# Turning keys and values for chunked linear attention: from TensorE transposes to VectorE block transposes and transfers

## The chip, the core and the metric

The kernel runs on one core of one Trainium2 chip. The metric is the device time of one launch in microseconds (us), lower is better; a time shown is the median of several runs. The engines of the core are TensorE (PE, its weight loads PEld), VectorE (DVE), ScalarE (ACT), GpSimd (POOL) and SyncE (SP, which issues transfers here).

## What is computed

One decoder layer for 1088 tokens (a prompt of 1024 and 8 samples of 8 tokens). Behind a norm, one projection gives queries, keys and values for eight heads of width 128: four retention heads (r0 to r3) and four mLSTM heads (m0 to m3). Each head runs over chunks of 128 tokens. For a retention head:

```
def step(S, inp):
    qc, kc, vc = inp
    scores = jnp.einsum('bhnd,bhmd->bhnm', qc, kc) * dmat[None]
    out = (jnp.einsum('bhnm,bhmv->bhnv', scores, vc)
           + jnp.einsum('bhnd,bhdv->bhnv', qc, S) * xi[None, :, :, None])
    S_new = (S * chunk_decay[None, :, None, None]
             + jnp.einsum('bhmd,bhmv->bhdv', kc * zeta[None, :, :, None], vc))
    return S_new, out
```

The mLSTM heads do the same with a running maximum, a gate per token and a normaliser. An output projection, norms and a gated feed-forward network with a causal convolution follow.

## The kernel before

All arithmetic is float32. A projection product is three matmuls on high and low parts (line 160), of 128 x 128 weights by 272 token columns; a tensor of 128 output columns (a query, key or value of one head) takes four quarters of 24 such matmuls. Projections leave a tensor with head dimension on partitions and tokens on the free axis (`q`, `k`, `v`, 128 x 1088). The chunk matmuls need keys and values the other way round, with the tokens of a chunk on partitions. So `front` handles two chunks at a time: TensorE transposes the two key chunks (L632) and the two value chunks (L633) into one PSUM tile `x`, VectorE scales the keys from there into `kz` (L636 for m heads, L640 for r heads), ScalarE scales the values into `vts` (L644), and TensorE makes the scores `s` (L666). `pt` (L669, L672) is the masked score. `u` (L774) is the key-value product of a chunk, `o` (L779, L781) the output, `S` (L785, L787) the running state. Chunks 0 to 7 are the prompt's; chunk 8 holds the samples.

The order of instructions on each engine comes from the Tile scheduler: the program is written head by head, and matmuls of the next head's projection stand between those of a pair of chunks. `proj` (L463) runs the projections, `evac_rot`, `evac_norm` and `evac_copy` bring their results out of PSUM; `last["row", b]` remembers the instruction that completed quarter b. `finish_previous` lets out the closing steps of the head before, ordered behind such an instruction. An r head from r1 on projects q, k, then v (r0 and r1 have their values from the start), an m head q, k, v. Weights come through SP into `st_in` and are split into `wh_in` and `wl_in` (L144, L146) some projections ahead. SP issues its transfers in order; a transfer whose source is not ready holds what stands behind it. Tiles that share a tag share a buffer in turn.

At the start the norms of the input run beside the first projections: ScalarE squares input tiles (L233), VectorE adds them (L235 to L237), TensorE sums over partitions (`ssqb_pm`, L210), ACT and DVE make the factor `rb` (L211 to L217) and scale the rotary tables `tab` with it (L310). The rotary step L500 on block 0 of `q_r0` then frees the PSUM bank that quarter 3 of r0's query projection, `in0_3`, writes next.

Of the kernel before, what the change touches and what calls it, by code (L numbers as in the profile page):

```python
# [16 lines left out]
P = 128  # L17
# [3 lines left out]
NB = 8  # L21
# [71 lines left out]
def hybrid_layer_kernel(ctx: ExitStack, tc: tile.TileContext, a: dict, o: dict):  # L93
# [166 lines left out]
    def tok(name, rows=P, dt=F32):  # L260
        return tokp.tile([P, T], dt, tag="tok", name=name)[:rows, :]
# [29 lines left out]
    sums = [m2.tile([P, NB, 129], F32, tag=t, bufs=1, name=f"sums_{t}").rearrange("p s v -> p (s v)") for t in ("vx", "sb")]  # L291
    sqs = [tok(f"sq{i}").rearrange("p (k n) -> p k n", k=4) for i in range(2)]
    for b in range(5):
# [31 lines left out]
        return out  # L325

    def spread_tile(name):
        return m2.tile([P, NB * 129], F32, tag="vx", bufs=1, name=name)

    rbd = dr.tile([1, T], F32, name="rbd")  # L330

# [36 lines left out]
        nc.scalar.activation(ig, ig, AF.Identity, bias=vec[0:NH, V_BG + 1:V_BG + 2])  # L368

    def gate_consts():  # L370
        xst = m2.tile([P, X_N], F32, tag="vx", bufs=1, name="xst")
# [87 lines left out]


    yT = []

    def proj(*jobs, mid=None, done=None, banks=lambda i, b: psA, pair=False):  # L463

# [29 lines left out]
    def evac_rot(t, name):  # L494
        def f(b, ps):
            o0, n = BLK[b]
            sw = m2.tile([P, Q], F32, tag="sw", name=f"sw_{name}{b}")[:, :n]
            nc.scalar.activation(sw[0:64, :], ps[64:128, :], AF.Copy)
            nc.scalar.activation(sw[64:128, :], ps[0:64, :], AF.Copy)
# [56 lines left out]
    def mix_head(hd, ml):  # L556
# [3 lines left out]
        if hid == 0:  # L560
            vs = [tok(f"v_r{i}") for i in range(2)]
            proj(*((i, evac_copy(t), w) for i, t, w in zip(first, vs, wv)),
                 banks=alternate, pair=True)
            early.extend(vs)
        v = early.pop(0) if early else tok(f"v_{nm}")
        q, k = tok(f"q_{nm}"), tok(f"k_{nm}")
        if ml:
            ub = ub_tile(f"ub{hd}")
            row = urows[hd:hd + 1, :]
            nc.sync.dma_start(ub, bass.AP(row.tensor, row.offset, [[0, P], [1, UB]]))  # L570
            proj((16 + hd, evac_norm(q, 1.0), split_w(staged.pop(), f"in{16 + hd}")))
            row = last["row", 3]
            proj((20 + hd, evac_norm(k, SCALE)), banks=alternate)
            finish_previous(2, row)
            proj((24 + hd, evac_copy(v)))
            finish_previous(1, last["row", 3])
            finish_previous(2, last["row", 3])
        else:
            eq, ek = evac_rot(q, f"q{nm}"), evac_rot(k, f"k{nm}")
            if hd == 0:  # L580
                proj((0, eq, split_to(stage_w(a["wi"][0], "in0"), *first_q)), mid=pre_norm, banks=lambda i, b: psB)
                here["wq"] = mp.tile([P, 2, 2, 2 * P], F32, tag="wq", name="wq")
                proj((NH, ek))
            else:
                proj((hd, eq))
                row = last["row", 3]
                proj((NH + hd, ek), banks=alternate)
                finish_previous(2, row)
                if hd == 1:
                    finish_previous(3, last["row", 1])  # L590
                    finish_previous(3, last["row", 2])
            if hd == 0:
                token_norms()
            if hd > 1:
                proj((2 * NH + hd, evac_copy(v)))
                finish_previous(1, last["row", 3])
                finish_previous(2, last["row", 3])
# [12 lines left out]
        if hid >= NH - 1:  # L610
            j = 12 + hid + 1 if hid + 1 < 2 * NH else 28
# [5 lines left out]
        dec = m2.tile([P, 8], F32, tag="dec", name=f"dec_{nm}")  # L617

        own = []

        def front(cs):

            c0, L = cs[0], len(cs)
            nmc = f"{nm}{c0}"
            px = bank(psB, 512, f"x_{nmc}").rearrange("p (j i n) -> p j i n", j=2, i=2)
            if c0 < 8:
                kc, vc = ([chunk(t, c) for c in cs] for t in (k, v))
            else:
                own.append(spread_tile(f"sp_{nm}"))
                kc, vc = ([spread_copy(t, own[0][:, i * P:(i + 1) * P])] for i, t in enumerate((k, v)))  # L630
            for i, c in enumerate(cs):
                nc.tensor.transpose(px[:, 0, i, :], kc[i], ident)  # L632
                nc.tensor.transpose(px[:, 1, i, :], vc[i], ident)  # L633
            kz = m2.tile([P, 2, P], F32, tag="kz", name=f"kz_{nmc}")
            if ml:
                nc.vector.tensor_tensor(kz[:, :L], px[:, 0, :L, :],  # L636
                                        cols[:, c0:c0 + L, NH + hd].unsqueeze(2).broadcast_to([P, L, P]), ALU.mult)
            else:
                zc = C_ZE + hd + (0 if c0 < 8 else NH)
                nc.vector.tensor_scalar(kz[:, :L], px[:, 0, :L, :], rc(zc, 1), None, ALU.mult)  # L640
# [915 lines left out]
```

## Time and profile before

| what | value |
|---|---|
| median of 3 runs | 1310.88 us (1310.76 to 1311.48) |
| the profiled execution's own time | 1311.53 us |
| its span in the trace | 1309.7 us |
| TensorE's mean granted clock | 0.997 of full speed |
| PE busy | 1296.0 us, 99% of the span |
| PEld / DVE / ACT / POOL busy | 98% / 76% / 46% / 33% |
| chain that ended last | PE 96%, DVE 2%, DMA 1%, ACT 1% |

The rows below come from the profiled execution, whose time is 0.65 us above the median. An engine's busy share is an average over stages; the stage tables and waits below tell which engine sets the pace where.

### The profile page before, as it was taken

The numbers are of one execution on the slowest core, as the hardware profiler recorded it, in microseconds if no ns is written. First come the engines' busy times: TensorE is split into PE (matmuls) and PEld (weight loads), VectorE is DVE, ScalarE is ACT, GpSimd is POOL, SyncE is SP. The second block draws the span as 40 slices with busy tenths as digits, with TensorE's granted clock in tenths as the row PEclk, the third lists the DMA queues.
The fourth block names the chain that finished last, engine by engine and source line by source line (L and its number), as shares of the span: only waits on it lengthen the run. The fifth ranks groups of instructions, "written<-read, shape, count | busy, mean of one in ns | idle before, by whom it ended". The sixth has DMA issues, their size and how long they took to land.

```text
span 1309.7 us, 26782 instructions
## 1 busy us (share of the span) xinstructions
PE 1296.0 (99%) x10501; PEld 1285.9 (98%) x10501; DVE 998.3 (76%) x2002; ACT 600.0 (46%) x1144; POOL 430.8 (33%) x564
## 2 busy tenths in 40 slices
PE   9999999999999999999999999999999999999996
PEld 9999999999999999999999999999999999999996
DVE  7774766657767655678999878787787888897678
ACT  7544433323433346455744434343443455543563
POOL 0354341758882000001334321222222214593002
PEclk9999999999999999999999999999999999999998
DMA  7344443567783124233144433444334469533363
GB/s 262 109 139 150 148 147 116 181 193 236 239 267 123 51 66 152 69 103 134 53 153 163 150 120 120 149 138 144 115 125 156 132 207 311 175 95 95 95 222 137
DMA packets 90784, 194.46 MB, mean 148 GB/s; under 512 B 13849, under 2 KB 39065, under 8 KB 90146
## 3 DMA queue, kind: packets, MB, share of 16 engines
q1 hardware_dynamic: 78210, 150.30, 34.4%
q0 software_dynamic: 12160, 41.95, 9.7%
q8 instruction: 82, 1.34, 0.4%
q10 hardware_dynamic: 288, 0.50, 0.1%
q14 instruction: 44, 0.36, 0.1%
HBM read 136.21 MB, written 56.50 MB: 147 GB/s over the span
## 4 chain that ended last, share of the span: by engine, by line
PE 96%; DVE 2%; DMA 1%; ACT 1%; issue 0%; SPq 0%
PE in L160 30%; PE out L160 7%; PE up_S L1130 6%; PE up_S L1129 6%; PE up_S L1128 6%; PE dn L1355 5%; PE dn L1356 5%; PE dn L1357 5%; PE up_A L1129 5%; PE up_A L1128 5%; PE up_A L1130 5%; PE up_A L1180 1%; PE up_A L1179 1%; PE up_A L1178 1%; DVE facc L1432 1%; PE s_r L666 1%
## 5 line engine op out<-in xcount | busy, mean ns | idle before, releaser
L160 PE MATMUL in<-hh,wh_in 128*128 128x272 f32 x960 | 277.8, 292 | 0.8 <-ACT hh L227 0.8
L160 PE MATMUL in<-hh,wl_in 128*128 128x272 f32 x960 | 277.4, 291 | 0.2 <-DVE wl_in L146 0.2
L160 PE MATMUL in<-hl,wh_in 128*128 128x272 f32 x960 | 277.1, 291 | 0.0
L160 PEld LDWEIGHTS in<-hh,wh_in 128*128 128x128 f32 x960 | 180.1, 188 | 2.8 <-issue 1.4
L160 PEld LDWEIGHTS in<-hh,wl_in 128*128 128x128 f32 x960 | 180.3, 188 | 1.4 <-issue 1.0
L160 PEld LDWEIGHTS in<-hl,wh_in 128*128 128x128 f32 x960 | 179.8, 188 | 0.9 <-issue 0.7
L144 ACT ACTIVATE wh_up<-st_up 128x1024 fp32r<-128x1024 f32 x84 | 80.5, 960 | 168.8 <-PE up_S L1129 97.1
L146 DVE TENSOR_TENSOR wl_up<-st_up,wh_up 128x1024 fp32r<-128x1024 f32 x84 | 96.0, 1144 | 9.9 <-ACT wh_up L144 9.9
L1102 DVE TENSOR_TENSOR Uv<-Uv,up_S 128x272 f32<-128x272 f32 (+1 forms) x200 | 66.4, 374 | 45.5 <-PE up_S L1130 45.5
L1283 DVE TENSOR_TENSOR rb<-rb 128x544 fp32r<-128x544 f32 x78 | 75.6, 974 | 28.7 <-ACT rb L1282 28.1
L1304 POOL TENSOR_TENSOR wd<-wd 128x512 f32<-128x512 f32 x44 | 74.5, 1715 | 47.0 <-DMA wd<-in_wd 20.0
L1282 ACT ACTIVATE rb<-rb 128x544 fp32r<-128x544 f32 x78 | 50.7, 651 | 82.2 <-DMA rb<-bd 71.2
L823 POOL TENSOR_TENSOR tab<-tab 128x256 f32<-128x256 f32 x104 | 79.1, 771 | 11.9 <-DMA tab<-in_wu 7.4
L1163 POOL TENSOR_TENSOR act<-act 128x544 f32<-128x544 f32 x40 | 63.4, 1586 | 58.0 <-DMA bd<-act 36.2
L1093 POOL MEMSET Ug<- 128x2 f32 x22 | 2.2, 99 | 221.5 <-DMA xr<-in_x 100.2
L1143 DVE SCALAR_TENSOR_TENSOR c<-Uv,vec,c 128x1024 f32<-128x1024 f32 (+1 forms) x88 | 68.5, 783 | 8.5 <-ACT c L1141 8.5
L1143 DVE SCALAR_TENSOR_TENSOR c<-Ug,vec,c 128x1024 f32<-128x1024 f32 x88 | 69.1, 825 | 0.0
L823 POOL TENSOR_TENSOR wq<-wq 128x256 f32<-128x256 f32 x56 | 47.8, 863 | 45.8 <-DMA wq<-in_wu 43.6
L144 ACT ACTIVATE wh_in<-st_in 128x1024 fp32r<-128x1024 f32 (+2 forms) x31 | 31.9, 1028 | 57.0 <-PE in L160 56.1
L1141 ACT ACTIVATE c<-Ug,vec 128x1024 f32<-128x1024 f32 (+1 forms) x44 | 34.6, 834 | 45.5 <-DVE Ug L1106 43.9
L823 POOL DMA_DIRECT2D tab<-in_wu x52 | 36.8, 713 | 33.1 <-DVE k_r L500 21.7
L1130 PE MATMUL up_S<-T1h,wl_up 128*128 128x272 f32 x160 | 46.4, 290 | 0.0
(557 smaller groups left out, 4652.8 us busy)
## 6 DMA issues: line engine op xcount, KB each, us to landing
rb<-bd SPq DMA_DIRECT2D x76, 272.0 KB, 2.8
st_up<-sd SPq DMA_DIRECT2D x40, 512.0 KB, 3.9
bd<-act SPq DMA_DIRECT2D x33, 544.0 KB, 3.3
st_in<-in_wi SPq DMA_DIRECT2D x31, 512.0 KB, 3.8
tab<-in_wu POOLq DMA_DIRECT2D x52, 256.0 KB, 5.3
sd<-tab POOLq DMA_DIRECT2D x26, 512.0 KB, 3.6
st_up<-in_wu SPq DMA_DIRECT2D x24, 512.0 KB, 3.2
wd<-in_wd SPq DMA_DIRECT2D x44, 256.0 KB, 5.1
```

What stands on the lines that cost most here:

```text
L144: act = nc.scalar.activation(hi, x, AF.Copy)
L146: last["split"] = act, eng.tensor_tensor(lo, x, hi.bitcast(F32), ALU.subtract)
L160: last["product", b] = nc.tensor.matmul(ps, u[:, k * P:(k + 1) * P], x[b // 2][k // 4][v][:, k % 4, qcols(b)], start=k == term == 0, stop= ...
L823: last["sums"] = f(*args)
L1102: nc.vector.tensor_tensor(o_, o_ if x is None else c(x), c(ps), ALU.add)
L1128: nc.tensor.matmul(ps, wh[:, c], xh[:, k, n], start=k == 0, stop=False)
L1129: nc.tensor.matmul(ps, wh[:, c], xl[:, k, n], start=False, stop=False)
L1130: nc.tensor.matmul(ps, wl[:, c], xh[:, k, n], start=False, stop=k == 3)
L1143: last["conv"] = nc.vector.scalar_tensor_tensor(c, u(i), cw(i), c, ALU.mult, ALU.add)
L1283: nc.vector.tensor_tensor(lo, x, hi.bitcast(F32), ALU.subtract)
L1304: last[out] = nc.gpsimd.tensor_tensor(quad(p, out), quad(p, x), quad(p, y), op)
L1355: nc.tensor.matmul(t, wh[:, ms], ah, start=k == 0, stop=False)
```

## The change

Chunks 0 to 7 of keys and values are no longer transposed by TensorE. `flip` does it when a projection's odd quarter is out of PSUM: for a half of 512 tokens VectorE transposes 32 x 32 blocks (L474 of the changed kernel), SP writes the result (256 KB) to a bounce buffer in DRAM (L475), and after the second half SP reads it back in four transfers of 32 partitions (128 KB each, in runs of 512 bytes, L479), which put every block in its final place: values back into `v`, keys into a new tile `kt` (for m heads the place in `yT` that the head's output takes later). The scaling of keys into `kz` (L670, L675) and of values into `vts` (L680) reads these tiles instead of PSUM. `kz` is ordered behind the query's last quarter on VectorE, and for r heads `vts` behind the query's last quarter on ScalarE. The sample chunk 8 is still transposed by TensorE.

R heads from r2 on now project k, v, q, r1 k, q, and m heads k, v, q; the closing steps of the head before are let out at other points, the weights are loaded in the new order, and some tiles have other buffers (`xst` and one of the `sums` tiles move, `ub` shares with `kt`). Over the whole program TensorE has 128 transposes fewer, VectorE 32 block transposes more, and SP 96 transfers more (32 writes, 64 reads); the numbers of ACT's and POOL's instructions stay. From the projection `in29` on, every engine's order is as it was.

```diff
+    def flip(dst, src, name):
+        bounce = dr.tile([2, P, CH4], F32, tag="bounce", bufs=4, name=f"bounce_{name}")
+        def f(b):
+            if b % 2 == 0:
+                return
+            half = slice(b // 2 * CH4, (b // 2 + 1) * CH4)
+            x = src[:, half]
+            d = m2.tile([P, CH4], F32, tag="flip", bufs=1, name=f"flip_{name}{b // 2}") if dst is src else dst[:, half]
+            nc.vector.transpose(d.rearrange("p (j c b) -> p c j b", j=4, c=4), x.rearrange("p (c j a) -> p c j a", c=4, j=4))
+            nc.sync.dma_start(bounce[b // 2], d)
+            if b == 3:
+                rows_ = bounce.rearrange("h (i a) n -> a (h i) n", i=4)
+                for j in range(4):
+                    nc.sync.dma_start(dst[32 * j:32 * j + 32, :8 * P].rearrange("p (g n) -> p g n", g=8),
+                                      rows_[:, :, j * P:(j + 1) * P])
+        return f
...
         if ml:
...
-            proj((16 + hd, evac_norm(q, 1.0), split_w(staged.pop(), f"in{16 + hd}")))
+            proj((20 + hd, evac_norm(k, SCALE), split_w(staged.pop(), f"in{20 + hd}")), done=flip_k)
             row = last["row", 3]
-            proj((20 + hd, evac_norm(k, SCALE)), banks=alternate)
+            proj((24 + hd, evac_copy(v)), banks=alternate, done=flip(v, v, f"v_{nm}"))
             finish_previous(2, row)
-            proj((24 + hd, evac_copy(v)))
-            finish_previous(1, last["row", 3])
-            finish_previous(2, last["row", 3])
+            finish_previous(3, row)
+            proj((16 + hd, evac_norm(q, 1.0)), banks=alternate)
+            finish_previous(3, last["row", 0])
...
-            for i, c in enumerate(cs):
-                nc.tensor.transpose(px[:, 0, i, :], kc[i], ident)
-                nc.tensor.transpose(px[:, 1, i, :], vc[i], ident)
...
             if ml:
-                nc.vector.tensor_tensor(kz[:, :L], px[:, 0, :L, :],
-                                        cols[:, c0:c0 + L, NH + hd].unsqueeze(2).broadcast_to([P, L, P]), ALU.mult)
+                with tc.issue_after(kz_after[c0 // 4].ins) if c0 < 8 else nullcontext():
+                    nc.vector.tensor_tensor(wide(kz[:, :L]), kx, cols[:, c0:c0 + L, NH + hd].unsqueeze(2).unsqueeze(3)
+                                            .broadcast_to([P, L, 4, 32]), ALU.mult)
...
-                nc.scalar.activation(vt[:, i, :P], px[:, 1, i, :], AF.Copy, scale=rcol[:, c:c + 1])
+                with tc.issue_after(vts_after[c0 // 4].ins) if c0 < 8 and not ml else nullcontext():
+                    nc.scalar.activation(vt[:, i, :P].rearrange("p (i b) -> p i b", i=4), vx[:, i], AF.Copy, scale=rcol[:, c:c + 1])
```

The order of the engines shows three places. The first is the start of the program, in the stretch that leads to the rotary step on `q_r0`'s block 0. VectorE's rows there before:

```order
L235 TENSOR_TENSOR sq0_143<-sq0_143,sq1_144 128x1088
L212 TENSOR_SCALAR rb_84<-ssqb_pm0_498 128x272
L236 TENSOR_TENSOR sq0_143<-sq0_143 128x544
L215 SCALAR_TENSOR_TENSOR sums_sb_142<-sums_sb_142,rb_84 128x272
L217 SCALAR_TENSOR_TENSOR rb_84<-sums_sb_142 128x272
L146 TENSOR_TENSOR wl_in12_843<-st_in12_840,wh_in12_842 128x1024
L310 TENSOR_TENSOR tab_81<-tab_81,rb_84 128x272 x2
L212 TENSOR_SCALAR rb_84<-ssqb_pm1_539 128x272
L500 TENSOR_TENSOR q_r0_467<-in0_0_473,tab_81 128x272
```

And VectorE's rows of the same stretch in the changed kernel, whose L525 is the rotary step:

```order
L474 STREAM_TRANSPOSE flip_v_r11_482<-v_r1_256 128x4x4x32
L212 TENSOR_SCALAR rb_84<-ssqb_pm0_522 128x272
L235 TENSOR_TENSOR sq0_141<-sq0_141,sq1_142 128x1088
L215 SCALAR_TENSOR_TENSOR sums_1_144<-sums_1_144,rb_84 128x272
L236 TENSOR_TENSOR sq0_141<-sq0_141 128x544
L217 SCALAR_TENSOR_TENSOR rb_84<-sums_1_144 128x272
L146 TENSOR_TENSOR wl_in12_875<-st_in12_872,wh_in12_874 128x1024
L310 TENSOR_TENSOR tab_81<-tab_81,rb_84 128x272 x2
L212 TENSOR_SCALAR rb_84<-ssqb_pm1_563 128x272
L525 TENSOR_TENSOR q_r0_489<-in0_0_497,tab_81 128x272
```

The first L212 went ahead of L235, and a block transpose ahead of both. ScalarE's rows that feed this stretch, before:

```order
L233 ACTIVATE sq1_144<-x3_106 128x1088
L233 ACTIVATE sq0_143<-x3_106 128x1088
L498 ACTIVATE sw_qr00_508<-in0_0_473 64x272
L499 ACTIVATE sw_qr00_508<-in0_0_473 64x272
L211 ACTIVATE sums_sb_142<-ssqb_pm0_498,eps_69 128x272
L213 ACTIVATE sums_sb_142<-sums_sb_142 128x272
L214 ACTIVATE sums_sb_142<-sums_sb_142 128x272
```

And ScalarE's rows there in the changed kernel:

```order
L233 ACTIVATE sq1_142<-x3_106 128x1088
L523 ACTIVATE sw_qr00_532<-in0_0_497 64x272
L524 ACTIVATE sw_qr00_532<-in0_0_497 64x272
L211 ACTIVATE sums_1_144<-ssqb_pm0_522,eps_69 128x272
L213 ACTIVATE sums_1_144<-sums_1_144 128x272
L233 ACTIVATE sq0_141<-x3_106 128x1088
L214 ACTIVATE sums_1_144<-sums_1_144 128x272
```

The last square, which L235 on VectorE reads, went behind four other ScalarE instructions.

The second place is the start of head m1's chunks on TensorE (`yt` are transposes of the finished head's output, `in18` and `in22` projections of m2). Before:

```order
L710 MATMUL yt_m0s_4485<-cst_80,on_m0s_4045 128x128
L632 MATMUL x_m10_4495<-cst_80,k_m1_4077 128x128
L633 MATMUL x_m10_4495<-cst_80,v_m1_4075 128x128
L632 MATMUL x_m10_4495<-cst_80,k_m1_4077 128x128
L633 MATMUL x_m10_4495<-cst_80,v_m1_4075 128x128
L666 MATMUL s_m10_4511<-q_m1_4076,k_m1_4077 128x128 x2
L632 MATMUL x_m12_4516<-cst_80,k_m1_4077 128x128
L633 MATMUL x_m12_4516<-cst_80,v_m1_4075 128x128
L632 MATMUL x_m12_4516<-cst_80,k_m1_4077 128x128
L633 MATMUL x_m12_4516<-cst_80,v_m1_4075 128x128
L666 MATMUL s_m12_4532<-q_m1_4076,k_m1_4077 128x128 x2
```

In the changed kernel the same place reads:

```order
L746 MATMUL yt_m0s_4509<-cst_80,on_m0s_4049 128x128
L702 MATMUL s_m10_4530<-q_m1_4080,k_m1_4081 128x128 x2
L702 MATMUL s_m12_4546<-q_m1_4080,k_m1_4081 128x128 x2
L160 MATMUL in22_0_4756<-hh_00_145,wh_in22_4752 128x272
L160 MATMUL in22_0_4756<-hh_00_145,wl_in22_4753 128x272
```

The eight transposes are gone; 19 matmuls of `in22` then stand ahead of the first `u`, where 23 of `in18` stood.

The third place is SP's order around the turned tensors of m1 in the changed kernel:

```order
L790 DMA out_cs<-sb_m0_3844 1024x1x128
L475 DMA bounce_k_m1_4082<-yT2_845 128x512
L644 DMA sb_m1_4515<-in_sc 128x8x128
L646 DMA sb_m1_4515<-in_sn 128x8x1
L132 DMA st_in26_4869<-in_wi 128x1024
L479 DMA yT2_845<-bounce_k_m1_4082 32x8x128 x4
L475 DMA bounce_v_m1_4201<-flip_v_m10_4260 128x512
L475 DMA bounce_v_m1_4201<-flip_v_m11_4315 128x512
L132 DMA st_in18_5047<-in_wi 128x1024
L479 DMA v_m1_4079<-bounce_v_m1_4201 32x8x128 x4
L132 DMA st_in23_5180<-in_wi 128x1024
```

Before, `out_cs`, the two loads of `sb` and three weight loads stood there and nothing else; the bounce's writes and reads now stand between them.

## Rows read from the trace of the kernel before

**Rows 1.** Busy us of each engine by stretch, with its instructions, TensorE's clock, DMA share, GB/s.

```profile
340.00:388.00 48.00, 48.00 (x408) 47.34 (x408) 33.75 (x105) 17.70 (x54) 40.96 (x58) 1.00 0.75 245
...
436.00:495.00 59.00, 59.00 (x495) 58.34 (x493) 40.43 (x123) 26.04 (x61) 0.00 (x0) 1.00 0.17 56
```

**Rows 2.** What TensorE waited for, in us, times and longest, the longest of four rows.

```profile
PE ssqb_fin L210 <- ACT facc_sq L1367: 1.3, 1, 1.3
```

**Rows 3.** The chain that ended last, at m1's first chunks: start us, us, what.

```profile
337.90 0.87 PE in L160 x7
...
339.32 0.11 PE x_m L632
...
339.76 0.45 PE s_m L666 x4
...
341.09 2.90 PE in L160 x23
343.99 0.44 PE u_m L774 x4
```

**Rows 4.** The lines of the transposes: ns min/median/max, first and last start in us.

```profile
L632 PE MATMUL x_r<-cst,k_r x32: 272/273/273, 110.4 to 251.6; 128*128 128x128 f32 x32
...
L632 PE MATMUL x_m<-cst,k_m x32: 272/272/273, 291.2 to 443.9; 128*128 128x128 f32 x32
```

**Rows 5.** Timeline of DVE at the start: start us, us, instruction.

```profile
35.79 1.29 DVE L235 TENSOR_TENSOR sq<-sq,sq 128x1088 f32<-128x1088 f32 x1 [0.86 <-ACT sq L233]
37.13 0.44 DVE L212 TENSOR_SCALAR rb<-ssqb_pm 128x272 f32<-128x272 f32 x1
37.49 0.72 DVE L236 TENSOR_TENSOR sq<-sq 128x544 f32<-128x544 f32 x1
...
41.60 0.42 DVE L500 TENSOR_TENSOR q_r<-in,tab 128x272 f32<-128x272 f32 x1
```

**Rows 6.** Timeline of ACT there.

```profile
33.65 2.11 ACT L233 ACTIVATE sq<-x 128x1088 f32<-128x1088 f32 x2
35.78 0.39 ACT L498 ACTIVATE sw_qr<-in 64x272 f32<-64x272 f32 x1
...
37.59 0.43 ACT L214 ACTIVATE sums_sb<-sums_sb 128x272 f32<-128x272 f32 x1
```

**Rows 7.** Timeline of PE there, end of in0_0 and first matmul of in0_3.

```profile
35.09 0.29 PE L160 MATMUL in<-hl,w_wq 128*128 128x272 f32 x1
...
42.42 0.49 PE L160 MATMUL in<-hh,w_wq 128*128 128x272 f32 x1
```

**Rows 8.** DVE's groups by shape: busy us, mean ns, idle before and its releaser.

```profile
L146 DVE TENSOR_TENSOR wl_in<-st_in,wh_in 128x1024 fp32r<-128x1024 f32 x29 | 36.4, 1255 | 5.0 <-ACT wh_in L144 4.6
...
L146 DVE TENSOR_TENSOR wl_up<-st_up,wh_up 128x512 fp32r<-128x512 f32 x20 | 14.6, 730 | 0.0
```

**Rows 9.** ACT's groups by shape, values out of PSUM and their scaling.

```profile
L644 ACT ACTIVATE vts<-x_m,rcol 128x128 f32<-128x128 f32 x36 | 11.4, 365 | 10.3 <-DVE kz_m L636 9.6 <-DVE mv_m L681 0.7
...
L484 ACT ACTIVATE v_m<-in 128x272 f32<-128x272 f32 x16 | 6.3, 396 | 31.2 <-PE in L160 31.2
```

**Rows 10.** DVE lines with two SBUF inputs (L659) and with a PSUM input (L636).

```profile
L659 DVE TENSOR_TENSOR wq<-wq,q_m x16: 385/422/1330, 258.7 to 447.0; 128x256 f32<-128x256 f32 x16
...
L636 DVE TENSOR_TENSOR kz_m<-x_m,cols x20: 249/414/426, 292.2 to 446.6; 128x256 f32<-128x256 f32 x16, 128x128 f32<-128x128 f32 x4
```

**Rows 11.** DMA issues: KB each, median us to landing (page, and 290 to 440 us).

```profile
bd<-act SPq DMA_DIRECT2D x11, 272.0 KB, 2.6
...
out_ss<-sb_r SPq DMA_DIRECT2D x4, 512.0 KB, 3.5
...
tab<-in_wu POOLq DMA_DIRECT2D x36, 256.0 KB, 5.8
```

**Rows 12.** One SP line's issue of transfers: ns, first and last start.

```profile
L754 SPq DMA_DIRECT2D out_ss<-sb_r x4: 570/580/667, 141.2 to 264.2; - x4
```

**Rows 13.** What SP waited for: us, times, longest.

```profile
SPq L614 <- DMA out_cs<-sb_m: 21.1, 3, 9.3
```

More of the change, by code (lines that the diff above doesn't have):

```diff
@@ L290, in hybrid_layer_kernel @@
     split_piece(0)
-    sums = [m2.tile([P, NB, 129], F32, tag=t, bufs=1, name=f"sums_{t}").rearrange("p s v -> p (s v)") for t in ("vx", "sb")]
     sqs = [tok(f"sq{i}").rearrange("p (k n) -> p k n", k=4) for i in range(2)]
+    sums = [tok("sums_0"), m2.tile([P, NB, 129], F32, tag="sb", bufs=1, name="sums_1").rearrange("p s v -> p (s v)")]
     for b in range(5):
@@ L327, in spread_tile @@
     def spread_tile(name):
-        return m2.tile([P, NB * 129], F32, tag="vx", bufs=1, name=name)
+        return m2.tile([P, 4 * 129], F32, tag="vx", bufs=1, name=name)
     rbd = dr.tile([1, T], F32, name="rbd")
@@ L370, in gate_consts @@
     def gate_consts():
-        xst = m2.tile([P, X_N], F32, tag="vx", bufs=1, name="xst")
+        xst = m2.tile([P, 4 * 129], F32, tag="vx", bufs=1, name="xst")[:, :X_N]
         nc.sync.dma_start(xst, a["cx"])
@@ L461, in hybrid_layer_kernel, with flipped @@
     yT = []
+    CH4 = 4 * P
+    def flip(dst, src, name):
[14 more added lines that the diff above has]
+        return f
+    def flipped(t, c, L):
+        c0 = c % 4
+        return t[:, c // 4 * CH4:(c // 4 + 1) * CH4].rearrange("p (i c b) -> p c i b", i=4, c=4)[:, c0:c0 + L]
     def proj(*jobs, mid=None, done=None, banks=lambda i, b: psA, pair=False):
@@ L498, in f @@
             nc.scalar.activation(sw[0:64, :], ps[64:128, :], AF.Copy)
-            nc.scalar.activation(sw[64:128, :], ps[0:64, :], AF.Copy)
+            last["sw", b] = nc.scalar.activation(sw[64:128, :], ps[0:64, :], AF.Copy)
             nc.vector.tensor_tensor(t[:, o0:o0 + n], ps, rot[0][:, o0:o0 + n], ALU.mult)
@@ L562, in mix_head @@
             proj(*((i, evac_copy(t), w) for i, t, w in zip(first, vs, wv)),
-                 banks=alternate, pair=True)
+                 banks=alternate, pair=True,
+                 done=lambda b, fs=[flip(t, t, f"v_r{i}") for i, t in enumerate(vs)]: [f(b) for f in fs])
             early.extend(vs)
@@ L566, in mix_head @@
         q, k = tok(f"q_{nm}"), tok(f"k_{nm}")
+        kt = yT[hid // 2][:, hid % 2] if ml else ub_tile(f"kt_{nm}")
+        flip_k = flip(kt, k, f"k_{nm}")
         if ml:
@@ L582, in mix_head @@
                 here["wq"] = mp.tile([P, 2, 2, 2 * P], F32, tag="wq", name="wq")
-                proj((NH, ek))
+                proj((NH, ek), done=flip_k)
             else:
-                proj((hd, eq))
+                proj((NH + hd, ek), done=flip_k)
                 row = last["row", 3]
-                proj((NH + hd, ek), banks=alternate)
-                finish_previous(2, row)
                 if hd == 1:
-                    finish_previous(3, last["row", 1])
-                    finish_previous(3, last["row", 2])
+                    proj((hd, eq), banks=alternate)
+                    finish_previous(2, row)
+                    finish_previous(3, row)
+                    finish_previous(3, last["row", 0])
             if hd == 0:
@@ L594, in mix_head @@
             if hd > 1:
-                proj((2 * NH + hd, evac_copy(v)))
-                finish_previous(1, last["row", 3])
-                finish_previous(2, last["row", 3])
+                proj((2 * NH + hd, evac_copy(v)), banks=alternate, done=flip(v, v, f"v_{nm}"))
+                finish_previous(2, row)
+                finish_previous(3, row)
+                proj((hd, eq), banks=alternate)
+                finish_previous(3, last["row", 0])
             if hd == 0:
@@ L610, in mix_head @@
         if hid >= NH - 1:
-            j = 12 + hid + 1 if hid + 1 < 2 * NH else 28
+            j = 16 + hid + 1 if hid + 1 < 2 * NH else 28
             staged.append(stage_w(a["wi"][j], f"in{j}"))
@@ L619, in mix_head @@
         own = []
+        kz_after, vts_after = ([last[kind, b] for b in (3,3)] for kind in ("row", "sw"))
         def front(cs):
@@ L624, in front @@
             nmc = f"{nm}{c0}"
-            px = bank(psB, 512, f"x_{nmc}").rearrange("p (j i n) -> p j i n", j=2, i=2)
+            wide = lambda t: t.rearrange("p c (i b) -> p c i b", i=4)
             if c0 < 8:
-                kc, vc = ([chunk(t, c) for c in cs] for t in (k, v))
+                kx, vx = flipped(kt, c0, L), flipped(v, c0, L)
+                kc = [chunk(k, c) for c in cs]
             else:
@@ L630, in front @@
                 kc, vc = ([spread_copy(t, own[0][:, i * P:(i + 1) * P])] for i, t in enumerate((k, v)))
-            for i, c in enumerate(cs):
-                nc.tensor.transpose(px[:, 0, i, :], kc[i], ident)
-                nc.tensor.transpose(px[:, 1, i, :], vc[i], ident)
+                px = bank(psB, 2 * P, f"x_{nmc}").rearrange("p (j n) -> p j n", j=2)
+                nc.tensor.transpose(px[:, 0, :], kc[0], ident)
+                nc.tensor.transpose(px[:, 1, :], vc[0], ident)
+                kx, vx = (wide(px[:, i:i + 1, :]) for i in range(2))
             kz = m2.tile([P, 2, P], F32, tag="kz", name=f"kz_{nmc}")
             if ml:
-                nc.vector.tensor_tensor(kz[:, :L], px[:, 0, :L, :],
-                                        cols[:, c0:c0 + L, NH + hd].unsqueeze(2).broadcast_to([P, L, P]), ALU.mult)
+                with tc.issue_after(kz_after[c0 // 4].ins) if c0 < 8 else nullcontext():
+                    nc.vector.tensor_tensor(wide(kz[:, :L]), kx, cols[:, c0:c0 + L, NH + hd].unsqueeze(2).unsqueeze(3)
+                                            .broadcast_to([P, L, 4, 32]), ALU.mult)
             else:
                 zc = C_ZE + hd + (0 if c0 < 8 else NH)
-                nc.vector.tensor_scalar(kz[:, :L], px[:, 0, :L, :], rc(zc, 1), None, ALU.mult)
+                with tc.issue_after(kz_after[c0 // 4].ins) if c0 < 8 else nullcontext():
+                    nc.vector.tensor_scalar(wide(kz[:, :L]), kx, rc(zc, 1), None, ALU.mult)
             vt = vts[0]
```

## The prediction

> **What bounds the kernel now.** I read the stage table first. In both stretches shown, one with POOL busy and one with POOL idle, TensorE is busy for the whole stretch (48.00 of 48, 59.00 of 59 us) at a granted clock of 1.00, and VectorE for about 70% of it [rows 1]. Next the waits of TensorE: four rows in the whole program, the longest 1.3 us [rows 2]. So the path is TensorE's instruction stream from start to end, and an instruction taken out of it should give back its spacing, unless something then comes late. Last the chain at m1's first chunks: it runs through TensorE without a break, and each transposed chunk is a piece of 0.11 us on it [rows 3]. The 0.27 us that a record shows for such a transpose [rows 4] is its length in a pipeline, not what it costs.
>
> **What is removed.** Line 632 has 32 transposes of prompt keys in the r heads and 32 in the m heads [rows 4]; line 633 has as many of values, which agrees with the 128 fewer instructions of the order. 128 x 0.11 = 14.1 us. The spacing is rounded, so 0.107 to 0.113 gives 13.7 to 14.5. From `in29` on the order is unchanged, and TensorE was full there, so nothing later gives this back by itself.
>
> **What the start loses.** TensorE's `in0_3` writes the bank that the rotary step on `q_r0`'s block 0 frees. Before, that step ended at 41.60 + 0.42 = 42.02 [rows 5] and `in0_3` began at 42.42 [rows 7]: 0.4 us to spare. VectorE ran from L235 at 35.79 to 42.02 without a hole, 6.2 us. In the changed order one instruction of this run, the first L212, stands ahead of L235; it is worth 37.49 - 37.13 = 0.36, so 5.9 us remain from L235 to the end of the rotary step. But L235 waits for ScalarE's last square, as it did before [rows 5], and that square now stands behind four others. Before, two squares took 33.65 to 35.76 [rows 6], 1.05 each. Now the first ends at 34.7; then `sw_qr00` needs `in0_0`, whose last matmul ends at 35.09 + 0.29 = 35.4 [rows 7]; the four instructions from L498 to L213 took 37.59 - 35.78 = 1.8 [rows 6], so they end at 37.2, and the square at 38.3. 38.3 + 5.9 = 44.2: `in0_3` would stand until then, **1.8 us later** than now. The waits at either end of this sum are worth some tenths, so I take 1.7, with 1.0 to 2.2 as bounds. What VectorE's block transposes cost doesn't enter: they stand in the 2.5 us that VectorE waits for the square. Behind the stall the same rows follow in the same spacing, so what comes next is shifted and not later still.
>
> **What VectorE and ScalarE get.** 32 block transposes of 128 x 512. No row shows one; the nearest are VectorE's passes over 128 x 512 (0.73) and 128 x 1024 (1.26) [rows 8]. At 1.0 they are four per head, 4 us in a period of 48 in which VectorE has 14 idle [rows 1], and nothing of TensorE's waits for them but by way of the transfers below. Scaling of keys and values keeps its number; its source changes from PSUM to SBUF. `kz` stands behind the query's last quarter, and TensorE's first `u` comes 0.9 (scores) + 2.4 (19 matmuls at 2.90 / 23 = 0.126) = 3.3 us later [rows 3]. VectorE has two `kz` ahead of that, 0.41 each [rows 10], and ends about 2 us before it is needed. Nothing is charged; without this cover one head would lose what `kz` takes.
>
> **What the transfers must hold.** The tightest is the value of heads r2, r3 and m0 to m3. Let T be the end of TensorE's last quarter of v. Its way: out of PSUM 0.4 [rows 9], block transpose 0.7 to 1.3: T+1.1 to 1.7. A write of 256 KB took 2.6 in the row nearest to it (272 KB written to DRAM), 5.8 for 256 KB in the stretch where POOL transfers [rows 11]: T+3.7 to 7.5. Between the write and the reads SP has a weight load (`st_in18` for m1), whose buffer comes free with `wl_in22` right behind the transposes, hence before the write has landed. Four reads of some 0.58 each to issue [rows 12] are 2.3, and landing takes 3.5 by the row with the same 512-byte runs [rows 11]; SP's longest wait for a transfer of that kind was 9.3, where POOL is busy [rows 13]. That makes T+9.5 at best and T+19.1 at worst; with a write of 4.2 it is **T+11.3**, my value, since three of the six heads run where POOL has ended or eases.
>
> It is needed for the first `u`: behind T stand the query's 96 matmuls (12.1), some nine transposes of the finished head (1.0), the scores (0.9) and 19 matmuls (2.4): T+16.4, and ScalarE takes 2 x 0.365 [rows 9] ahead of it: **T+15.6**. So 4.3 us are to spare. Keys have one projection more (12 us) everywhere but in r1, where the key is needed near T+19 of its own and its reads land as above. The key's reads stand behind `out_cs` and its landing wait, 9.3 at the longest [rows 13], which that projection covers. Behind the waiting reads stand weight loads for a projection two or more ahead, with a whole head's period to spare. What POOL does later (it waited for the rotary tables' last use) has an idle stretch of 59 us before it is needed [rows 1].
>
> **The sum.** 14.1 - 1.7 = 12.4. Against the profiled execution, 1311.53 - 12.4 = 1299.1; that execution is 0.65 above the median of the runs shown, so the median should be **1298.5 us**.
>
> **Rivals.**
> (a) The start costs nothing or little, because ScalarE gets to the last square early enough or `in0_3` has more slack than the trace shows. For it: the slack is read off pipelined records. Against it: the sum above misses by over a microsecond only if the order of rows is not the order of execution. 1311.53 - 14.1 - 0.65 = 1296.8.
> (b) VectorE's `kz` for the m heads gets stretched. It was a pass with one input in PSUM and never took over 0.43, while L659, a pass of the same size with two inputs in SBUF, took 0.385 to 1.33 [rows 10], and the long ones lie where POOL computes. The changed `kz` has two SBUF inputs. Four in a head, each longer by up to 1.33 - 0.41 = 0.92, are 3.7 at worst against about 2 to spare: 1.7 in each of m0 to m2, 5.1 in all: 1303.6. Against it: L659's median is 0.42, so the likely stretch is hidden.
> The Trainium skill (SBUF — State Buffer, section Who interferes with whom) says that a VectorE instruction with two SBUF inputs contends with a GpSimd instruction that reads SBUF, and one with a single SBUF input doesn't; the trace agrees in these two lines, and by the rule every `kz` of m0 to m2 may be hit, which is this rival's upper price.
> (c) The values' reads land late in the heads with POOL busy. At T+19.1 they miss T+15.6 by 3.5, three times, 10.5: 1309.0. For it: the DMA share is already 0.75 in that stretch [rows 1], and each head adds 2 MB there. Against it: needs the longest wait seen in all three.
> (d) Slower than before. The same mechanism in all six heads: the saved 12.4 is spent when the reads land 2.1 us late in each, at T+17.7, and the kernel is measurably slower from T+18.1; at T+19.1 in all six it is 21.0 lost: 1319.5. Against it: from 436 us on the DMA share is 0.17 [rows 1], and in r2, r3 and m3 nothing in the rows shows a long landing.
> That the change does not do what it says, and the transposes stay, is excluded by the order.
>
> **Chances.** The forecast 0.64, (a) 0.14, (b) 0.08, (c) 0.08, (d) 0.06. The range reaches from (a)'s lower side, 14.5 saved and nothing lost, 1311.53 - 14.5 - 0.65 = 1296.4, up to 1306.0, which holds (b) whole and half of (c). The likeliest case's own range is 1297.5 to 1300. A change within 0.2% (2.6 us) is about what a measurement can't tell from none: (c) and (d) where they nearly meet the gain make 0.03 of it. Faster 0.91, same 0.03, slower 0.06.
>
> **What would show it.** No `x` transposes but the samples', and TensorE still busy throughout; a wait of TensorE's `in` line for VectorE's `q_r` of 1 to 2.2 us near 42 us; s and u of m1 some 0.9 us closer together; no wait of `u` for ScalarE's `vts`, with the values' reads landing 4 us ahead. A wait of `vts` for a transfer that reaches TensorE would show (c) or (d); waits of `u` for `kz`, with `kz` above 0.43 where POOL computes, would show (b). A block transpose of over 2 us would upset nothing in the sum but use half of the slack.

## The result, and the profile after

The changed kernel is slower: median 1330.80 us (four runs, 1329.19 to 1336.51) against 1310.99 of the kernel before beside it; the ratio is 1.0158, with a 95% interval of 1.0127 to 1.0190. The forecast was 1298.5. The profiled execution took 1331.95 us, its span is 1330.1.

The busy line of the page, TensorE's granted clock and the DMA engines' busy share in 40 slices of the span, of the changed kernel:

```profile
PE 1294.6 (97%) x10373; PEld 1281.2 (96%) x10373; DVE 1018.5 (77%) x2034; ACT 601.6 (45%) x1144; POOL 436.6 (33%) x564
...
PEclk9999999989898999999999999999999999999998
DMA  7543565788886423323144434434344359533363
```

TensorE is busy for only 1.4 us less than before (1296.0), though it has 128 instructions fewer, and the span is longer; the clock, which before stood at full speed in every slice but the last, dips in slices 9, 11 and 13, in or just behind the slices in which the DMA engines are busiest. The busy table by stretch (columns as in [rows 1]):

```profile
200.00:292.00 92.00, 88.27 (x728) 86.48 (x727) 59.83 (x186) 26.57 (x77) 43.77 (x60) 0.98 0.70 207
...
340.00:388.00 48.00, 39.53 (x308) 37.47 (x308) 38.11 (x108) 14.98 (x48) 41.54 (x55) 0.93 0.79 251
388.00:436.00 48.00, 41.73 (x329) 40.30 (x328) 28.02 (x93) 16.33 (x48) 24.31 (x33) 0.93 0.69 206
436.00:495.00 59.00, 59.00 (x495) 58.34 (x494) 37.67 (x135) 22.76 (x57) 0.00 (x0) 1.00 0.32 94
```

Where TensorE had been busy for 48.00 of 48 us [rows 1], it now stands for 8.5 us in 340 to 388 and for 6.3 in the next stretch, and the granted clock is 0.93 in the mean of both. From 436 us on, with POOL idle, nothing is lost. The largest waits of TensorE in the changed kernel (us in total, times, longest), where before the longest in the whole program was 1.3 [rows 2]:

```profile
PE yt_m0s L746 <- DVE on_m0s L743: 6.3, 1, 6.3
PE yt_m1s L746 <- DVE on_m1s L743: 4.6, 1, 4.6
PE u_m L810 <- ACT vts L680: 3.1, 1, 3.1
PE yt_r3s L746 <- DVE on_r3s L743: 2.9, 1, 2.9
```

They name what came last at TensorE: the closing steps of the head before, which stand behind something on VectorE, and the scaled values. The samples' update `us_m` is the last act of every m head on TensorE, so the end of its row dates the end of m3. After, and before:

```profile
L778 PE MATMUL us_m<-sp_m,kz_m x32: 376/428/480, 312.2 to 472.9; 32*128 32x258 f32 x32
```

```profile
L742 PE MATMUL us_m<-sp_m,kz_m x32: 376/428/480, 308.4 to 453.0; 32*128 32x258 f32 x32
```

Behind it both kernels take the same time to the end of the span (1330.1 - 472.9 = 857.2, 1309.7 - 453.0 = 856.7). So the whole difference lies ahead of it: m3 should have ended at 453.0 - 14.1 = 438.9 and ended at 472.9, **34.0 us late**. Of these, TensorE stood still for 22.3 (the holes of the stretches from 110 to 436 us), and about 9.4 went in work at a lower clock. Here is how this looks in m1 (2 us to a row):

```profile
342.00:344.00 2.00, 1.00 (x8) 0.78 (x7) 2.00 (x2) 0.00 (x0) 1.20 (x2) 1.00 0.45 170
344.00:346.00 2.00, 0.00 (x0) 0.00 (x0) 1.90 (x8) 0.40 (x1) 1.49 (x3) 1.00 0.44 121
346.00:348.00 2.00, 0.00 (x0) 0.00 (x0) 1.57 (x6) 0.61 (x3) 1.90 (x3) 0.65 0.85 247
348.00:350.00 2.00, 0.69 (x3) 0.70 (x4) 1.93 (x6) 0.00 (x0) 1.76 (x3) 0.50 1.12 367
350.00:352.00 2.00, 2.00 (x11) 2.00 (x11) 1.52 (x5) 0.00 (x0) 1.86 (x3) 0.50 0.99 257
352.00:354.00 2.00, 2.00 (x12) 2.00 (x12) 0.00 (x0) 0.00 (x0) 0.54 (x2) 0.64 1.10 315
```

TensorE has had no work since 343 us. From 347 on the granted clock is 0.50, which is the lower of its two levels, 1.2 of 2.4 GHz; work comes back at 349.3, and up to about 353 it runs at half speed. The same follows the standstills of m0 and m2. Summing busy time times the missing share of the clock over such rows gives the 9.4.

**One head's chain.** VectorE in m1: the two block transposes of the value's halves, and the first evacuation of a query quarter behind them:

```profile
329.15 0.70 DVE L474 STREAM_TRANSPOSE flip_v_m<-v_m 128x512 f32<-128x512 f32 x1
341.89 0.71 DVE L474 STREAM_TRANSPOSE flip_v_m<-v_m 128x512 f32<-128x512 f32 x1 [12.04 <-DMA bounce_v_m<-flip_v_m]
...
344.20 0.43 DVE L515 SCALAR_TENSOR_TENSOR q_m<-in,rb 128x272 f32<-128x272 f32 x1
```

SP there:

```profile
319.25 0.32 SPq L475 DMA_DIRECT2D bounce_k_m<-yT  x1
325.02 0.55 SPq L644 DMA_DIRECT2D sb_m<-in_sc  x1
...
326.45 3.00 SPq L132 DMA_DIRECT2D st_in<-in_wi  x1
329.90 3.64 SPq L479 DMA_DIRECT2D yT<-bounce_k_m  x4
333.59 9.38 SPq L475 DMA_DIRECT2D bounce_v_m<-flip_v_m  x2
...
344.79 2.99 SPq L479 DMA_DIRECT2D v_m<-bounce_v_m  x4
```

ScalarE there, the value's last quarter out of PSUM and the first scaling of the turned value:

```profile
330.10 0.40 ACT L509 ACTIVATE v_m<-in 128x272 f32<-128x272 f32 x1 [2.62 <-PE in L160]
...
354.10 1.87 ACT L680 ACTIVATE vts<-v_m,rcol 128x128 f32<-128x128 f32 x6 [6.96 <-DMA v_m<-bounce_v_m]
```

And two stretches of the chain that ended last, the writes of the two halves and then the landing of the reads:

```profile
333.59 8.18 DMA bounce_v_m<-flip_v_m
...
342.63 2.11 DMA bounce_v_m<-flip_v_m
```

```profile
346.19 7.89 DMA v_m<-bounce_v_m
```

Read from the top: TensorE's last quarter of v ends at 330.1. The first block transpose is at 329.15, but its write is issued only at 333.59, since SP first issues the key's four reads, which themselves came late behind the two loads of the state and a weight load. The write takes 8.2 us. **The second block transpose waits for it for 12.04 us**, because both halves of a value go through the one `flip` tile (one buffer): the second may not overwrite it before the first has been read out. Everything behind it on VectorE waits too, the query's evacuations and the closing steps of m0's samples among it. TensorE ends the query's matmuls at 343.0; its next instruction is `yt_m0s`, which reads `on_m0s`, and VectorE writes that only at 348.55 to 349.25. So TensorE stands from 343.0 to 349.3, the 6.3 us of the row above. Then come the second write (2.1), the reads and their landing, and the value is there at 354.1, which is 24.0 us behind its last quarter; the forecast had 11.3, and 15.6 was needed.

### The profile page after: what moved, and what is told of

Its sections match the earlier page's. It is cut to its first block, busy times and chain, and to the rows that moved or that the text cites. A ratio compares the mean times of both kernels' runs of the same rounds, so it can differ in the third digit from the quotient of the medians.

```text
span 1330.1 us, 26737 instructions
## 1 busy us (share of the span) xinstructions
PE 1294.6 (97%) x10373; PEld 1281.2 (96%) x10373; DVE 1018.5 (77%) x2034; ACT 601.6 (45%) x1144; POOL 436.6 (33%) x564
## 4 chain that ended last, share of the span: by engine, by line
PE 82%; DMA 7%; DVE 6%; SPq 1%; ACT 1%; issue 1%; POOL 1%; DVEq 0%; ACTq 0%; POOLq 0%
PE in L160 19%; PE out L160 7%; PE up_S L1166 6%; PE up_S L1165 6%; PE up_S L1164 6%; PE dn L1391 5%; PE dn L1392 5%; PE dn L1393 5%; PE up_A L1165 5%; PE up_A L1164 5%; PE up_A L1166 5%; DMA bounce_v_m<-flip_v_m 2%; DMA v_m<-bounce_v_m 2%; SPq L479 1%; PE up_A L1216 1%
## 5 line engine op out<-in xcount | busy, mean ns | idle before, releaser
L1319 DVE TENSOR_TENSOR rb<-rb 128x544 fp32r<-128x544 f32 x78 | 78.5, 1011 | 28.7 <-ACT rb L1318 26.8
L859 POOL TENSOR_TENSOR tab<-tab 128x256 f32<-128x256 f32 x104 | 82.6, 805 | 17.5 <-DMA tab<-in_wu 13.0
L146 DVE TENSOR_TENSOR wl_in<-st_in,wh_in 128x1024 fp32r<-128x1024 f32 (+2 forms) x31 | 38.3, 1236 | 22.2 <-ACT wh_in L144 22.2
```

Of the source, the lines that this page charges most:

```text
L146: last["split"] = act, eng.tensor_tensor(lo, x, hi.bitcast(F32), ALU.subtract)
L859: last["sums"] = f(*args)
L1319: nc.vector.tensor_tensor(lo, x, hi.bitcast(F32), ALU.subtract)
```

## The experiments

The theory after this reading (A): the one tile makes the second half's transpose wait for the first half's write, and VectorE with it. Rivals: (B) the key's transfers stand ahead of the value's in SP's order and in the queue; (C) the DMA engines are full in the stretches in which POOL loads and writes the sums of the feed-forward weights, and any transfer of the value is late. The table puts all runs together. "Ideal" is the kernel before beside it, less 0.11 us for each transpose that is gone (an estimate: the spacing of [rows 3] is rounded). The last three columns are, for m0, m1 and m2, the us from the value's last quarter to its first scaling on ScalarE, of the profiled execution.

```
kernel                      median   ratio, 95%             ideal    lost   m0    m1    m2
changed                     1330.80  1.0158 1.0127-1.0190   1296.9   33.9   23.6  24.0  22.4
two places for values       1317.47  1.0047 1.0032-1.0062   1297.0   20.5   13.1  20.5  22.9
keys only                   1304.86  0.9953 0.9939-0.9968   1304.1    0.8    -     -     -
values only                 1315.46  1.0042 1.0028-1.0056   1304.1   11.4   15.4  14.0  18.3
fewer loads by POOL         1315.18  1.0028 1.0008-1.0048   1297.0   18.2   16.7  17.7  14.0
key's reads earlier on SP   1328.49  1.0124 1.0106-1.0142   1297.1   31.4   20.9  25.1  21.2
two places, reads earlier   1315.58  1.0038 1.0024-1.0052   1297.1   18.5   18.8  17.8  21.6
 the same, fewer loads      1302.86  0.9937 0.9925-0.9950   1297.1    5.8   13.5  13.4  13.2
values only, two places     1307.01  0.9972 0.9960-0.9984   1304.7    2.3   12.1  13.5  16.4
keys, values of r0-2, m3    1303.57  0.9944 0.9932-0.9956   1300.7    2.9    -     -     -
keys, values of r0, r1      1303.38  0.9946 0.9932-0.9959   1302.9    0.5    -     -     -
```

**Two places for the values.** The values of m0 to m2 are transposed into half of an output tile that no head uses yet:

```diff
-            d = m2.tile([P, CH4], F32, tag="flip", bufs=1, name=f"flip_{name}{b // 2}") if dst is src else dst[:, half]
+            d = dst[:, half] if dst is not src else via[:, half] if via is not None else m2.tile([P, CH4], F32, tag="flip", bufs=1, name=f"flip_{name}{b // 2}")
...
-            proj((24 + hd, evac_copy(v)), banks=alternate, done=flip(v, v, f"v_{nm}"))
+            proj((24 + hd, evac_copy(v)), banks=alternate,
+                 done=flip(v, v, f"v_{nm}", yT[(hid + 1) // 2][:, (hid + 1) % 2] if hd < 3 else None))
```

> The values of m0 to m2 are transposed into a free half of the next heads' output tile instead of the one flip tile, so their two halves have two places; all else stays. Theory A, the one flip tile (VectorE waits 9 to 12 us in each of these heads for the first half's write to land, with the query's evacuations behind it): the wait goes, both writes go out together, 1300 to 1308. Rival B, the transfers themselves (the value's write is issued behind the key's four reads and lands 6 to 8 us later, the reads take as long again): the values still land some 18 to 21 us behind the last quarter where 15.6 is needed, 1312 to 1322.

1317.5: 13.3 us come back, and 20.5 stay lost, so neither theory holds alone. The waits of TensorE in this kernel no longer name VectorE's closing steps:

```profile
PE u_m L811 <- ACT vts L681: 11.7, 2, 7.1
```

ScalarE in its m1, last quarter and first scaling:

```profile
318.24 0.40 ACT L509 ACTIVATE v_m<-in 128x272 f32<-128x272 f32 x1 [2.62 <-PE in L160]
...
338.71 1.86 ACT L681 ACTIVATE vts<-v_m,rcol 128x128 f32<-128x128 f32 x6 [13.66 <-DMA v_m<-bounce_v_m]
```

The value still arrives 20.5 us behind its last quarter: both writes are out at once now, and land late. TensorE, which nothing else stops here, shows when it needed the value:

```profile
339.17 1.23 PE L811 MATMUL u_m<-vts,kz_m 128*128 128x129 f32 x4 [4.63 <-ACT vts L681]
```

It had been waiting since 334.54, 16.3 us behind the last quarter.

**Keys only, and values only.** In the first, `front` transposes the values on TensorE again, in the second the keys; the projections keep the new order (the calls of `flip` that go with it aren't shown):

```diff
...
-                kx, vx = flipped(kt, c0, L), flipped(v, c0, L)
-                kc = [chunk(k, c) for c in cs]
+                kx = flipped(kt, c0, L)
+                kc, vc = ([chunk(t, c) for c in cs] for t in (k, v))
+                px = bank(psB, 2 * P, f"x_{nmc}").rearrange("p (i n) -> p i n", i=2)
+                for i, c in enumerate(cs):
+                    nc.tensor.transpose(px[:, i, :], vc[i], ident)
+                vx = wide(px)
```

> Values go through TensorE again (64 transposes are back, 7.0 us), keys stay with block transposes and transfers, in the new order of projections. If the key's way has no cost on the path (A and B): 1310.9 - 7.0 = 1304, no wait of TensorE in the heads, clock 1.00. If the extra traffic or the new order alone costs time: above 1307.

1304.9, against an ideal of 1304.1: turning the keys by transfers gives all that their 64 transposes were worth, and the new order costs nothing, within the interval of some 2 us. In the stretches of m1 and m2 (columns as in [rows 1]) TensorE is nearly full again, with the DMA engines at 0.83 and 0.85:

```profile
292.00:340.00 48.00, 48.00 (x407) 47.34 (x407) 37.24 (x107) 17.61 (x53) 42.61 (x55) 1.00 0.83 258
340.00:388.00 48.00, 47.19 (x390) 45.58 (x389) 37.54 (x104) 16.69 (x50) 42.75 (x56) 1.00 0.85 266
```

> Keys go through TensorE again (7.0 us back), values stay with block transposes, the one flip tile and transfers. Theory A with a hold that doesn't depend on the keys: about 10 us lost in each of m0 to m2 as now, 1325 to 1338. Rival B (the value's write is slow because the key's reads stand ahead of it): the write lands in 2 to 4 us, VectorE waits no longer than that, values land near 13 us behind the last quarter: 1303 to 1309.

1315.5, between the two: 11.4 lost with half the extra traffic. The hold of VectorE by the value's first write (total, times, longest), in the changed kernel and then in this one:

```profile
DVE flip_v_m L474 <- DMA bounce_v_m<-flip_v_m: 32.4, 3, 12.0
```

```profile
DVE flip_v_m L474 <- DMA bounce_v_m<-flip_v_m: 16.0, 3, 7.9
```

Without the key's transfers the hold is halved, to 5.3 in the mean. That speaks for B or C beside A, and the two can be told apart in part. In the changed kernel 2.9, 3.7 and 4.9 us of the holds of m0 to m2 (9.2, 12.0, 11.1) lie ahead of the write's issue, in SP's order. Here the write is issued right behind the transpose in all three heads, in m1 behind one that ran from 321.68 to 322.38:

```profile
322.40 7.69 SPq L475 DMA_DIRECT2D bounce_v_m<-flip_v_m  x2
```

So 11.5 of the 16.4 us by which the hold shrank were time in SP's order (B), and 4.9 lay between issue and landing.

**Fewer loads by POOL.** From the second stretch of the sums on, this kernel leaves out their loads after the first three; it computes other feed-forward results than the layer's and is there for its time alone.

```diff
-                if 0 < ahead and i + ahead < i1:
+                if 0 < ahead and i + ahead < min(i1, i0 + len(tiles)):
```

> POOL's sums of the feed-forward weights keep their additions and their writes, but from the second stretch on they leave out their loads after the first three, so they add stale data and the later results are not the layer's; all of the attention part is as changed. Rival C, the DMA engines being full (busy share 0.9 to 1.07 in the stretches of the stalls) while POOL loads: with a good part of that traffic gone writes and reads take 2 to 4 us, as they do in m3 now, 1297 to 1305. If the single tile or SP's order holds things up by itself: still 1318 or more.

1315.2: 15.6 us come back, less than a full C would give; its ten runs scatter, from 1309.1 to 1319.8. The one tile still holds VectorE here, for 15.4 us in the three heads.

**The key's reads earlier on SP.** The load of the head's state and a weight load are ordered behind the key's reads:

```diff
...
+        with tc.issue_after(turned[f"k_{nm}"].ins):
             nc.sync.dma_start(sb[:, :, :P], a["sc" if ml else "sr"][hd].rearrange("p (s v) -> p s v", s=NB))
...
+            with tc.issue_after(turned[f"k_m{hd - 1}" if hd else "k_r3"].ins):
+                st_v = stage_w(a["wi"][24 + hd], f"in{24 + hd}")
```

> Only SP's order changes: the key's four reads go ahead of the load of the head's state and of a weight load a head ahead, so they are done before the value's write is issued. The one flip tile stays. If the hold of VectorE is long because the value's write stands behind the key's reads (B): the first write lands in 2 to 5 us, the hold falls from 9 to 12 to about 5 us a head, 1314 to 1321. If the write is slow for other traffic, with or without the key's reads ahead: no change, 1326 to 1333.

1328.5, an interval that overlaps that of the changed kernel: this order of SP gives back nothing that can be told from noise. It doesn't refute B, though. In m0 and m2 no part of the hold lies ahead of the write's issue any more, and it fell to 7.0 and 7.4 us. In m1 the write now stood behind the loads that had been moved, and the hold rose. The sum of the three is as before:

```profile
330.89 9.56 SPq L476 DMA_DIRECT2D bounce_v_m<-flip_v_m  x2
...
339.39 0.71 DVE L475 STREAM_TRANSPOSE flip_v_m<-v_m 128x512 f32<-128x512 f32 x1 [16.42 <-DMA bounce_v_m<-flip_v_m]
```

```profile
DVE flip_v_m L475 <- DMA bounce_v_m<-flip_v_m: 30.8, 3, 16.4
```

The first half was turned at 322.97, and 7.9 us went by until its write was issued. So what SP's order costs by itself stays untested: no kernel here keeps the key's transfers and POOL's loads and lets the value's write go out first in every head.

> Two places for the values of m0 to m2, and the key's reads ahead in SP's order. If these two are the whole cause: the values land near 13 us behind the last quarter, TensorE waits at most 1 us a head, 1298 to 1305. If the traffic of the stage by itself makes writes and reads slow (C): the values still land later than 15.6 in some heads, 1308 to 1317.

1315.6, as with two places alone within the noise. The next kernel is this one with the fewer loads of POOL:

> Two places, the key's reads ahead, and POOL's sums without most of their loads (they add stale data, so the feed-forward results are not the layer's). All three suspects are taken away: 1297 to 1300, the full 14 us. If more is lost, a fourth cause is open.

1302.9, short of the 1297 to 1300 expected: another 12.7 come back, and in all three heads the value is scaled 13.2 to 13.5 us behind its last quarter, ahead of the 15.6. The write's median landing from 290 to 436 us (KB each, us), with POOL's loads and then without:

```profile
bounce_v_m<-yT SPq DMA_DIRECT2D x4, 256.0 KB, 9.2
```

```profile
bounce_v_m<-yT SPq DMA_DIRECT2D x4, 256.0 KB, 5.6
```

Two places save 13.3 with the loads and 12.3 without them (the latter together with SP's order), and fewer loads save 15.6 with one place and 12.7 with two: the two causes nearly add, as far as the scatter of the one-place kernel allows. 5.8 us stay unexplained in this kernel; TensorE's waits in its heads are under 1 us each, and its holes from 110 to 480 us add up to 2.5.

**Values only, with two places.** The values-only kernel with the edit of the first experiment:

> Keys go through TensorE again (7.0 us back), values by transfers with two places in m0 to m2. The rest of the cost in the two-places kernel (1317.5, 20 us over its ideal) is then either the key's own 16 transfers' traffic or POOL's loads. If the key's traffic is most of it: values land near 13 us, 1304 to 1307. If POOL's loads alone make the values late: 1309 to 1316, no better than with one tile (1315.5).

1307.0, 2.3 off the ideal: with the key's transfers gone, the second place is worth 8.5 us and POOL's loads alone make the values hardly late. ScalarE in m1, and TensorE's waits in the heads:

```profile
321.26 0.40 ACT L509 ACTIVATE v_m<-in 128x272 f32<-128x272 f32 x1 [2.62 <-PE in L160]
...
334.76 1.87 ACT L683 ACTIVATE vts<-v_m,rcol 128x128 f32<-128x128 f32 x6 [6.20 <-DMA v_m<-bounce_v_m]
```

```profile
PE s_m L705 <- ACT yT L757: 1.4, 1, 1.4
...
PE u_m L813 <- ACT vts L683: 0.7, 1, 0.7
```

So C is not POOL's loads alone but the sum: POOL's stream, the key's megabyte and the value's megabyte in one head's period. With POOL's loads, keys alone lose 0.8, values alone with two places 2.3, both together 20.5; both without most of the loads lose 5.8, with the key's reads moved too.

**Two mixtures.** Values go through TensorE where they were late (r3, m0 to m2), or everywhere but in r0 and r1:

```diff
+        by_pe = hid in (3, 4, 5, 6)
...
+                if by_pe:
+                    px = bank(psB, 2 * P, f"x_{nmc}").rearrange("p (i n) -> p i n", i=2)
+                    for i, c in enumerate(cs):
+                        nc.tensor.transpose(px[:, i, :], vc[i], ident)
+                    vx = wide(px)
```

> Keys stay turned by VectorE and transfers everywhere; values go through TensorE in r3 and m0 to m2, the heads that wait now, and by transfers in r0, r1, r2 and m3. 32 transposes come back: 96 x 0.11 = 10.6 are saved against the kernel before. If the late values of those four heads are all that costs: 1300 to 1302, no wait over 1 us in the heads. If keys and values elsewhere cost something too: 1304 or more.

> Keys are turned by VectorE and transfers in all heads, values that way in r0 and r1 alone, whose values are there long before they are used; the other values go through TensorE. 80 transposes are saved, 80 x 0.11 = 8.8: 1302.3 if nothing waits. Against the mixed kernel (1303.6, 1300.8 to 1307.0) it gives up 1.8 us and the transfers of r2's and m3's values: if these were what made its times scatter and cost about 3, it ends level with it, 1302 to 1304, with less scatter; if not, 1304.5 to 1306.

1303.6 and 1303.4: the first lies above the 1300 to 1302 hoped for, the second where it was expected; both beat the kernel before by 0.55%, and can't be told apart. The second leaves nothing on the table (0.5 off its ideal); in the stretches of m1 and m2 TensorE has no hole at all, though the DMA engines are at 0.84 and 0.86:

```profile
292.00:340.00 48.00, 48.00 (x407) 47.34 (x406) 37.01 (x108) 17.38 (x53) 42.14 (x55) 1.00 0.84 263
340.00:388.00 48.00, 48.00 (x408) 47.34 (x407) 35.18 (x116) 18.83 (x58) 39.92 (x55) 1.00 0.86 269
```

## Why the prediction was wrong, by its steps

**What bounds the kernel, and what is removed: right.** An instruction taken from TensorE gives back its 0.11 us. Keys only gave 6.3 of 7.0, the last mixture 8.4 of 8.8. The time at which the value is needed was right too: T+16.4 for the first `u` by the sum, 16.3 in m1 of the two-places kernel.

**What the start loses: wrong, by 1.7 us.** VectorE was late as worked out, by less; the rotary step of block 0 ends at 43.5. VectorE's rows of the changed kernel, L235 and that step, and TensorE's first matmul of `in0_3`:

```profile
37.78 1.29 DVE L235 TENSOR_TENSOR sq<-sq,sq 128x1088 f32<-128x1088 f32 x1 [1.02 <-ACT sq L233]
...
43.10 0.42 DVE L525 TENSOR_TENSOR q_r<-in,tab 128x272 f32<-128x272 f32 x1
```

```profile
41.98 0.49 PE L160 MATMUL in<-hh,w_wq 128*128 128x272 f32 x1
```

`in0_3` begins at 41.98, ahead of the end of that step, so it doesn't wait for it, and that step isn't what frees the bank, against what stands ahead of the prediction and in its sum. Which instruction does, the rows don't show. The stall is none; rival (a) was right in this term.

**What the transfers must hold: this is the step that failed,** in three of its terms. The first is "block transpose 0.7 to 1.3: T+1.1 to 1.7", which treats a value's two halves as if they could follow one another. The transposes themselves are cheap, as the row (ns min/median/max) shows:

```profile
L474 DVE STREAM_TRANSPOSE flip_v_m<-v_m x8: 698/708/712, 269.9 to 444.8; 128x512 f32<-128x512 f32 x8
```

But the second half waits for the first half's write, since `flip` has one buffer: T+11.8 in m1. The line that says so (`bufs=1`) is in the diff that I showed. With it goes "nothing of TensorE's waits for them but by way of the transfers": VectorE stood there in m1 with the query's evacuations and the closing steps of m0 behind it. Two places gave back 13.3 us.

The second is the landing: a write of 4.2 and reads of 3.5, priced from rows of a median, half of them outside the stage, and with 5.8 for the write's upper bound from a load of POOL's. Inside it, from 290 to 400 us, the changed kernel's rows are (KB each, us):

```profile
bounce_v_m<-flip_v_m SPq DMA_DIRECT2D x4, 256.0 KB, 5.1
v_m<-bounce_v_m SPq DMA_DIRECT2D x4, 128.0 KB, 6.0
```

In m1 the first write took 8.2, beyond my worst bound of 5.8; the reads took 9.3 from their first issue, where I had 2.3 + 3.5. The third is SP's order, which I charged between write and reads alone: the first write stood behind the key's reads and the loads ahead of them and was issued 3.5 us behind T. Together the value was there at T+22.4 to 24.0 in m0 to m2, beyond my worst T+19.1. I had rival (c) at 0.08, with the DMA share of 0.75 for it. That share is a mean over 48 us: in windows of 10 us from 250 to 410 the changed kernel's share lies between 0.63 and 1.07, and m1's first write lies in the fullest, 330 to 340.

**Rivals.** (d), slower by late values, is what happened, but not as I drew it: it needs no late value in all six heads. Three heads with a hold of 9 to 12 us each and what follows from it cost more than six that are 2 us late. r3 and m3 lost little, as said against it. (b) is small: with two inputs in SBUF `kz` is slower where POOL computes, 0.61 in the mean against a longest of 0.43 before [rows 10] (from 292 to 436 us, columns as in [rows 8]):

```profile
L670 DVE TENSOR_TENSOR kz_m<-yT,cols 128x256 f32<-128x256 f32 x10 | 5.9, 611 | 0.0
```

From 436 us on, where POOL is idle, the same pass takes 0.42 in the mean. The Trainium skill (SBUF — State Buffer, section Who interferes with whom) says that a VectorE instruction with two SBUF inputs contends with a GpSimd instruction that reads SBUF, and these two means agree with it. TensorE's waits name `kz` nowhere.

**The price of a standstill.** I priced a late value by its lateness. The runs show a second bill, the lower clock after the stop: 9.4 of the 34.0 us in the profiled execution.

Not settled: 2.3 of the 34.0, the 5.8 of the kernel with all three suspects gone, and how much of what the key's transfers cost the value is SP's order and how much is landing beside them. With one place 11.5 us of the hold lay ahead of the write's issue; with the key's reads moved it was 7.9, all of it in m1.

## What to carry to other kernels

Before a transfer that empties a scratch tile is called hidden, count that tile's buffers: with one buffer the next use waits for the whole landing, and on an engine that issues in order everything behind it waits as well. Price a new transfer by the landing times of the stage that it runs in, at their long end, and ask what the stage's DMA share becomes in its busy slices, not in the mean. Look also at what stands ahead of it in the issuing engine's order. And take the half of such a change that has slack: the keys, with two projections to land in, gave their full gain, the values with one did not.

## What the runs showed of the hardware

A block transpose of 128 x 512 float32 took 0.70 us on VectorE, no more than another pass over that size [rows 8]. At or just behind standstills of 2.9 to 6.3 us TensorE's granted clock fell from 1.00 to 0.50, and the first 3 to 6 us of work behind them ran at that level. A write of 256 KB to DRAM took from 2.0 us with POOL idle to over 8 in the stretch with POOL's loads and the key's reads, where a later one, m1's second, took 2.1.
